# The recurrences of the chunk inverses issued on GpSimd instead of VectorE

## The chip, the cores and the metric

One core of one Trainium2 chip. The metric is the device time of one execution in microseconds (us). Engines are named as in the profile: PE is TensorE, PEld its weight loads, DVE is VectorE, ACT is ScalarE, POOL is GpSimd, SP is SyncE, which here issues most DMAs.

## What is computed

One layer of a hybrid decoder for a prompt of 1024 tokens and 8 samples of 4 tokens. All columns come from one product `x @ w_in`. A part of them feeds RWKV-7 time mixing, 8 heads of 64, which the reference runs token by token:

```python
def step(S, inp):
    r_t, w_t, k_t, v_t, kk_t, a_t = inp
    sa = jnp.einsum('bhvk,bhk->bhv', S, -kk_t)
    S = (S * w_t[:, :, None, :] + sa[..., None] * (kk_t * a_t)[:, :, None, :]
         + v_t[..., None] * k_t[:, :, None, :])
    return S, jnp.einsum('bhvk,bhk->bhv', S, r_t)
```

The other columns feed dilated window attention, gates, two output products, a last product and a layer norm. The change touches the time mixing of the prompt alone.

## The kernel before

The kernel takes the recurrence in chunks of 64 tokens. Inside a chunk the steps depend on each other through a strictly triangular 64x64 matrix, and the kernel needs the inverse of identity plus that matrix. The work is cut into 8 units: 4 pairs of heads (`j`) by 2 halves of the tokens (`hf`). A unit has 8 chunks and 2 heads, so 16 triangular matrices. Five streams make the first stage of the program, up to about 563 us:

- `products`: the columns of `x @ w_in`. Each 128 columns take two loads of weights (`load_w`, line L165 the load into `wraw`, L168 on ACT and L169 on DVE the split into `whi` and `wlo`) and 72 matmuls (L178). This is what PE does most of the time.
- `unit`: prepares a unit. It ends, for what matters here, with the masked matrices `AT` (L392, DVE, from PSUM tiles `g` that the matmuls of L385 write).
- `inverse`: the 32x32 diagonal blocks of the triangular matrices go to DRAM and back with another layout (`Yd`, L448; `Y`, L451, both issued on SP), and so 128 partitions each hold one row of work. Then 31 steps of forward substitution, r = 0 to 30: a product `tm` (L457) and a subtraction from `X` (L460) over m = r//4 + 1 rows of n = 31 - r elements, from 31 elements in the first to 8 in the last, at most 76. Each of the 62 operations needs the one before. At the end `X` goes back to DRAM (`Xd`, L464).
- `scan`: reads the inverted blocks back into `AT` (L478, SP), transposes them with DVE into `T1` (L479; the profile writes it `T`), joins the halves with small matmuls (L492, L502), and then goes chunk by chunk through the state: matmul L543, `W` on DVE (L544), matmul L549, the new state `st` on DVE (L552).
- `norms`: the output norm of a unit.

Two things set the order. `run_streams` deals the streams' pieces out by due times (`D_INV`, `D_IN` and the like), and PE executes exactly in that order (`manual_schedule`). On the other engines and in the DMA queues a scheduler chooses the order by its own estimate of when each instruction is ready. Once chosen it is fixed: every engine and every queue executes its own list in order, and an instruction that waits holds up all that stand behind it.

PSUM is scarce: the tiles `g` and `sc` have two banks each, `pj` four.

Of the kernel before, what the change touches and what calls it, by code (L numbers as in the profile page):

```python
# [15 lines left out]
ALU = mybir.AluOpType  # L16
# [68 lines left out]
def tile_layer(ctx: ExitStack, tc: tile.TileContext, A: dict, O: list):  # L85
    nc = tc.nc
    V, S, G, T, SP = nc.vector, nc.scalar, nc.gpsimd, nc.tensor, nc.sync
# [10 lines left out]
    def mk(pool, shape, tag, bufs=None, dt=F32):  # L98
        uid[0] += 1
        return pool.tile(list(shape), dt, tag=tag, name=f"{tag}_{uid[0]}", bufs=bufs)  # L100
# [216 lines left out]
    def unit(j, hf, M, st, out):  # L317
# [45 lines left out]
            yield None  # L363
        Mr = M[0]
        E = mk(rp, [P, 8, 65], "E", 2)
        G.memset(E[:, :, 0:1], 1.0)
        S.activation(E[:, :, 1:65], lam.rearrange("p (a b) -> p a b", a=8), AF.Exp, scale=-0.5 * CDEC)
        Ev = E.rearrange("p (a b) c -> p a b c", b=2)
        KR = mk(rp, [P, 4, 4, 64], "KR", 2)
# [72 lines left out]
    def inverse(j, hf, AT, out):  # L442
        Yd = mk(dpool, [2, 2, 2, 4, 32, 32], f"Yd{j}{hf}")
        Xd = mk(dpool, [2, 2, 2, 4, 32, 32], f"Xd{j}{hf}")
        blk = lambda p, b, w: AT[64 * (1 - p) + 32 * b : 64 * (1 - p) + 32 * b + 32, w, p::2, 64 * (1 - p) + 32 * b : 64 * (1 - p) + 32 * b + 32]
        for p in range(2):
            for b in range(2):
                SP.dma_start(Yd[p, b].rearrange("e c j i -> j e c i"), blk(p, b, slice(0, 2)))  # L448
        Y = mk(rp, [P, 32, 32], "Y", 1)
        for q in range(4):  # L450
            SP.dma_start(Y[32 * q : 32 * q + 32], Yd.rearrange("p b e c j i -> (p b e c) j i"))  # L451
        X = mk(rp, [P, 8, 32], "X", 1)
        SP.dma_start(X[:], A["cst"][:, XI0:].rearrange("p (a b) -> p a b", a=8))
        for r in range(31):
            m, n = r // 4 + 1, 31 - r
            tm = mk(rp, [P, 80], "tm", 2)[:, 0 : m * n].rearrange("p (a b) -> p a b", a=m)
            V.tensor_tensor(  # L457
                tm, Y[:, r : r + 1, r + 1 : 32].to_broadcast([P, m, n]), X[:, 0:m, r : r + 1].to_broadcast([P, m, n]), ALU.mult
            )
            V.tensor_tensor(X[:, 0:m, r + 1 : 32], X[:, 0:m, r + 1 : 32], tm, ALU.subtract)  # L460
            if r % 2:
                yield (0.0, D_INV)
        for q in range(4):
            SP.dma_start(  # L464
                Xd.rearrange("p b e c (a q) i -> q (p b e c) a i", q=4)[q],
                X[32 * q : 32 * q + 32],
            )
        out.append((Xd, blk))
# [235 lines left out]
    def units():  # L704
        for u in range(8):
            j, hf = u // 2, u % 2
            while j not in pairs:
                yield None
            M, st = pairs[j]
            yield from unit(j, hf, M, st, ready)  # L710
            done["unit"] += 1
        while done["scan"] < 7:
            yield None
        yield from sample_rows()

    def inverses():
        for u in range(8):
            while len(masked) <= u:
                yield None
            yield 0.0, D_IN  # L720
            yield from inverse(*masked[u], inv)
            yield 0.0, D_UP
            done["inv"] += 1
# [753 lines left out]
```

## Time and profile before

| | |
|---|---|
| median of 3 runs | 1368.11 us (1365.16 to 1368.77) |
| the profiled execution | 1365.17 us, its span 1363.5 us, granted clock 0.993 |
| PE busy | 1331.7 us, 98% of the span |
| DVE busy | 804.4 us, 59% |
| ACT busy | 469.2 us, 34% |
| POOL busy | 67.0 us, 5% |
| L457 and L460 on DVE | 248 each, 210 and 209 ns |
| first and last of them | 77.3 us and 523.5 us |

The span is the time from the first to the last instruction, and 1.7 us of the execution lie around it. A timeline row reads: start, duration, engine (SPq means that SP's queue issues a DMA there, and the duration is the issue alone), line, operation, output <- inputs, shapes, count of merged instructions, and in brackets the idle time of the engine before it with what ended it. A row of waits reads: waiting engine and line, what it waited for, total us, times, longest.

### The profile page before, as it was taken

To read this page: it belongs to the slowest core of one execution; us is meant where nothing else is said; L and a number is where in the kernel's file an instruction comes from. 1 tells how busy PE (TensorE), PEld (TensorE's weight loads), DVE (VectorE), ACT (ScalarE), POOL (GpSimd) and SP (SyncE) were. 2 spreads that over 40 slices of the span, in tenths; PEclk is the share of its full clock that TensorE was granted. 3 is DMA by queue.
4 is the path that set the end of the run, shared out by engine and by line. 5 is a ranking of instruction groups with operands and counts; after the bars stand their busy time and mean duration, and the time that the engine had idled before them with its cause. 6 is when DMAs were issued, how large, how long until landed. Compare 5 with 4: busy or idle time off the path is not lost.

```text
span 1363.5 us, 25941 instructions
## 1 busy us (share of the span) xinstructions
PE 1331.7 (98%) x10101; PEld 1241.0 (91%) x10101; DVE 804.4 (59%) x2204; ACT 469.2 (34%) x1065; POOL 67.0 (5%) x82
## 2 busy tenths in 40 slices
PE   9999999999999999999999999999999999999997
PEld 7998999898988999999999999999999998899786
DVE  5677668786476855543554385437543844665565
ACT  5334344434443443422332323232332234132211
POOL 0000000000000000000000000000000000025100
PEclk9999999999999999999999999999999999899999
DMA  6122223122313233328545455555554666795221
GB/s 210 44 61 66 67 86 97 51 75 72 93 61 81 72 109 96 96 89 156 106 109 120 118 132 103 123 129 128 100 120 119 135 130 158 237 286 163 84 100 68
DMA packets 340151, 151.64 MB, mean 111 GB/s; under 512 B 188808, under 2 KB 329502, under 8 KB 339774
## 3 DMA queue, kind: packets, MB, share of 16 engines
q1 hardware_dynamic: 241150, 129.68, 35.0%
q10 hardware_dynamic: 98880, 20.32, 7.5%
q8 instruction: 79, 1.29, 0.4%
q14 instruction: 42, 0.34, 0.1%
HBM read 110.68 MB, written 38.97 MB: 110 GB/s over the span
## 4 chain that ended last, share of the span: by engine, by line
PE 82%; DVE 11%; DMA 3%; issue 1%; SPq 1%; ACT 1%; ACTq 0%; DVEq 0%
PE pj L178 60%; PE pj L1431 7%; PE o L985 2%; PE s L948 2%; DVE tm L457 1%; DVE X L460 1%; PE g L385 1%; PE t L968 1%; PE s L1067 1%; DMA wraw<-in_w_in_dram 1%; PE sc L543 1%; DMA cb<-cd 1%; DVE wlo L169 1%; DVE st L552 1%; PE sc L549 1%
## 5 line engine op out<-in xcount | busy, mean ns | idle before, releaser
L178 PE MATMUL pj<-xhi,whi 128*128 128x352 f32 x1848 | 398.3, 337 | 4.5 <-ACT xhi L1298 3.1
L178 PE MATMUL pj<-xhi,wlo 128*128 128x352 f32 x1848 | 386.1, 330 | 0.0
L178 PE MATMUL pj<-xlo,whi 128*128 128x352 f32 x1848 | 380.5, 327 | 0.0
L178 PEld LDWEIGHTS pj<-xhi,whi 128*128 128x128 f32 x1848 | 304.5, 190 | 20.7 <-issue 10.6
L178 PEld LDWEIGHTS pj<-xlo,whi 128*128 128x128 f32 x1848 | 309.2, 190 | 1.8 <-issue 0.7
L178 PEld LDWEIGHTS pj<-xhi,wlo 128*128 128x128 f32 x1848 | 307.1, 189 | 3.9 <-issue 2.3
L169 DVE TENSOR_TENSOR wlo<-wraw,whi 128x512 fp32r<-128x512 f32 x162 | 112.8, 697 | 89.6 <-ACT whi L168 88.8
L168 ACT ACTIVATE whi<-wraw 128x512 fp32r<-128x512 f32 x162 | 100.5, 625 | 132.5 <-PE pj L178 94.3
L958 ACT ACTIVATE Sm<-Sm,nm 128x128 f32<-128x128 f32 (+1 forms) x96 | 42.4, 442 | 101.8 <-DVE nm L955 101.8
L457 DVE TENSOR_TENSOR tm<-Y,X 128x60 f32<-128x60 f32 (+24 forms) x248 | 52.1, 210 | 10.5 <-DMA Y<-Yd 4.3
L460 DVE TENSOR_TENSOR X<-X,tm 128x60 f32<-128x60 f32 (+24 forms) x248 | 51.9, 209 | 6.0
L552 DVE SCALAR_TENSOR_TENSOR st<-sc,E,SD 64x64 f32<-64x64 f32 x128 | 36.1, 282 | 29.0 <-PE sc L549 27.3
L950 DVE CUSTOM_DVE_ANT_0 Sm<-s,cst 128x128 f32<-128x128 f32 (+1 forms) x96 | 29.2, 347 | 39.6 <-PE s L948 38.9
L1431 PE MATMUL pj<-wl,mh 128*128 128x512 f32 (+1 forms) x136 | 51.9, 382 | 0.0
L541 ACT ACTIVATE SD<-st,E 128x128 f32<-128x128 f32 x64 | 25.6, 401 | 70.5 <-DVE st L552 70.4
L811 POOL TENSOR_TENSOR kvp<-vv,kv 128x512 f32<-128x512 f32 x16 | 20.2, 1262 | 470.8 <-DVE Ss L819 386.7
L985 PE MATMUL o<-PT,Vt 128*128 128x128 f32 x280 | 38.7, 276 | 0.8 <-ACT PT L972 0.8
L948 PE MATMUL s<-k,q 128*128 128x128 f32 (+1 forms) x192 | 37.8, 326 | 1.1 <-DVE ml L950 1.1
L873 ACT ACTIVATE k<-pj 128x352 f32<-128x352 f32 (+1 forms) x36 | 16.2, 455 | 65.1 <-PE pj L178 60.9
L311 ACT ACTIVATE zt<-pj,der 128x352 f32<-128x352 f32 x48 | 26.5, 553 | 33.1 <-PE pj L178 27.8
L985 PEld LDWEIGHTS o<-PT,Vt 128*128 128x128 f32 x280 | 36.4, 191 | 1.5 <-ACT PT L972 1.1
L544 DVE TENSOR_TENSOR W<-sc,R 64x128 f32<-64x128 f32 x64 | 18.4, 288 | 29.5 <-PE sc L543 28.4
(325 smaller groups left out, 1699.4 us busy)
## 6 DMA issues: line engine op xcount, KB each, us to landing
wraw<-in_w_in_dram SPq DMA_DIRECT2D x146, 256.0 KB
gd<-zt SPq DMA_DIRECT2D x48, 176.0 KB
gt<-gd SPq DMA_DIRECT2D x48, 176.0 KB
vs<-bt ACTq DMA_DIRECT2D x48, 128.0 KB
kc<-in_cache_kv_g_dram SPq DMA_DIRECT2D x48, 128.0 KB
Vt<-vs ACTq DMA_DIRECT2D x12, 512.0 KB
cb<-cd SPq DMA_DIRECT2D x12, 512.0 KB
zd<-zt SPq DMA_DIRECT2D x24, 176.0 KB
```

The source lines that it names most:

```text
L168: S.activation(hi[:], raw[:], AF.Copy)
L169: V.tensor_tensor(lo[:], raw[:], hi.bitcast(F32)[:], ALU.subtract)
L178: T.matmul(out, w[wi][:, n % 4, :], x[:, n % 4, :], start=first and n == 0, stop=last and n == 11)
L311: S.activation(t[:], b[:], AF.Tanh, scale=0.5, bias=der[:, HB + col : HB + col + 1])
L457: V.tensor_tensor(tm, Y[:, r : r + 1, r + 1 : 32].to_broadcast([P, m, n]), X[:, 0:m, r : r + 1].to_broadcast([P, m, n]), ALU.mult)
L460: V.tensor_tensor(X[:, 0:m, r + 1 : 32], X[:, 0:m, r + 1 : 32], tm, ALU.subtract)
L552: V.scalar_tensor_tensor(S1[d, d], pS[d, d], E[d, c, 64:65], SD[d, d], ALU.mult, ALU.add)
L948: T.matmul(r, qT[:, i * P : (i + 1) * P], kT[:, keys[i][0] * P : keys[i][0] * P + n], start=True, stop=True)
L950: V.tensor_tensor_reduce(out=Sm[:, i, 0:n], in0=r, in1=m3 if g == 2 else m12[:, 256 - n : 256], scale=1.0, scalar=NEG, op0=ALU.add, op1=AL ...
L958: S.activation(Sm[:, i, 0:n], Sm[:, i, 0:n], AF.Exp, scale=SCALE, bias=nm[:, x : x + 1], accum_out=ml[:, g, 1, i : i + 1])
L985: T.matmul(po[:, (i % 4) * P : (i % 4 + 1) * P], st["Vt"][:, kb_, :], PT[:, n * P : (n + 1) * P], start=m == 0, stop=m == len(keys[i]) - 1,)
L1431: T.matmul(pb[:], a[:, k], wk, start=x == 0, stop=x == len(prods) - 1)
```

## The change

All 62 operations of each of the 8 inverses go to POOL. The clearing of the first column of `E`, a tile of the decays that `unit` builds (L366; the change's title calls what needs it kappa), goes from POOL to DVE.

```diff
-        G.memset(E[:, :, 0:1], 1.0)
+        V.memset(E[:, :, 0:1], 1.0)
...
         for r in range(31):
             m, n = r // 4 + 1, 31 - r
             tm = mk(rp, [P, 80], "tm", 2)[:, 0 : m * n].rearrange("p (a b) -> p a b", a=m)
-            V.tensor_tensor(
+            G.tensor_tensor(
                 tm, Y[:, r : r + 1, r + 1 : 32].to_broadcast([P, m, n]), X[:, 0:m, r : r + 1].to_broadcast([P, m, n]), ALU.mult
             )
-            V.tensor_tensor(X[:, 0:m, r + 1 : 32], X[:, 0:m, r + 1 : 32], tm, ALU.subtract)
+            G.tensor_tensor(X[:, 0:m, r + 1 : 32], X[:, 0:m, r + 1 : 32], tm, ALU.subtract)
```

PE's list is the same, row by row. The lists of DVE, SP and POOL change, and ACT's at a few places. First, DVE at the end of the first inverse, as a difference; a number behind a name tells one tile of that name from the next. `T_258_1425` is the first unit's `T1`, `AT_704` its matrices, `AT_1114` the second unit's matrices.

```order
-L457 TENSOR_TENSOR tm_1131<-Y_907,X_912 128x75
+L479 STREAM_TRANSPOSE T_258_1425<-AT_704 32x256
 L392 TENSOR_TENSOR AT_1114<-g_1150,cst_76 128x512
-L460 TENSOR_TENSOR X_912<-X_912,tm_1131 128x5x15
 L392 TENSOR_TENSOR AT_1114<-g_1151,cst_76 128x512
-L457 TENSOR_TENSOR tm_1134<-Y_907,X_912 128x70
-L460 TENSOR_TENSOR X_912<-X_912,tm_1134 128x5x14
-L457 TENSOR_TENSOR tm_1162<-Y_907,X_912 128x65
+L479 STREAM_TRANSPOSE T_258_1425<-AT_704 32x256
 L205 SCALAR_TENSOR_TENSOR zt_1176<-zt_1177,pj_1012 128x352
```

The transposes of the first unit now stand ahead of the last two maskings of the second unit; before, the recurrence was at its steps of 75 to 65 elements there, and the transposes came after its end.

Second, DVE at the third inverse. Before, the transposes of its unit (`T_545_2969`) stood here, after the second unit's whole loop over the chunks (`Ot_2343` is its output):

```order
L371 TENSOR_TENSOR KR_2922<-m_1235,E_2919 128x4x2x64
L564 TENSOR_TENSOR Ot_2343<-Ot_2343,g_2863 128x512
L574 TENSOR_REDUCE m_529_2898<-Ot_2343 128x8
L575 TENSOR_SCALAR m_529_2898<-m_529_2898 128x8
L576 TENSOR_TENSOR Ot_2343<-Ot_2343,m_529_2898 128x512
L479 STREAM_TRANSPOSE T_545_2969<-AT_2149 32x256
```

Now they stand inside that loop:

```order
L169 TENSOR_TENSOR wlo_2830<-wraw_2827,whi_2829 128x512
L552 SCALAR_TENSOR_TENSOR st_68_386<-sc_2675,E_1050,SD_2645 64x64 x2
L373 SCALAR_TENSOR_TENSOR t_2925<-m_1235,prm_96,t_2626 128x512
L479 STREAM_TRANSPOSE T_545_2969<-AT_2149 32x256
L544 TENSOR_TENSOR W_1205<-sc_2702,R_237_1303 64x128
L479 STREAM_TRANSPOSE T_545_2969<-AT_2149 32x256
L552 SCALAR_TENSOR_TENSOR st_67_385<-sc_2727,E_1050,SD_2700 64x64 x2
L544 TENSOR_TENSOR W_1205<-sc_2763,R_237_1303 64x128
```

`W` and `st` of the sixth to the eighth chunk of the second unit, which stood ahead of the transposes before, are behind them now. The other units are alike: the eighth unit's transposes now stand between `st` and `W` of the seventh unit's loop.

Third, SP's queue at the first inverse, as a difference:

```order
 L165 DMA wraw_1475<-in_w_in_dram 128x4x128
+L464 DMA Xd_149_902<-X_912 256x1x32 x4
 L165 DMA wraw_1581<-in_w_in_dram 128x4x128
+L478 DMA AT_704<-Xd_149_902 32x8x32 x4
 L206 DMA zd_95<-zt_1141 128x352
+L453 DMA X_1617<-in_cst_dram 128x256
 L448 DMA Yd_281_1606<-AT_1114 32x8x32 x2
```

The transfers of the finished `X` went ahead of a load of weights, of the stores `zd` and of the second unit's `Yd`, behind which they stood before. On POOL the eight inverses follow each other; between them stand only the clearings of `st` for the third and fourth pair (L681, after the third and the fifth inverse) and, after the sixth, three operations of the sample rows (L631, L646, L647).

## The prediction

> **What bounds the kernel now.** I read the page first, then the windows of the first stage, then PE's waits, then the timeline around single inverses. The page:
>
> ```profile
> PE 1331.7 (98%) x10101; PEld 1241.0 (91%) x10101; DVE 804.4 (59%) x2204; ACT 469.2 (34%) x1065; POOL 67.0 (5%) x82
> ```
>
> PE bounds the whole. The next fence has two stretches, that of the eight inverses and the third inverse's 30 us: length, busy time of PE, PEld, DVE, ACT and POOL, clock, DMA share and rate. Then the same for tile X alone (DVE), and PE's waits in the long stretch.
>
> ```profile
> 77.00:525.00 448.00, 434.37 (x3936) 405.71 (x3935) 321.48 (x1124) 187.97 (x397) 2.83 (x14) 0.99 0.27 76
> 194.00:224.00 30.00, 28.98 (x213) 27.30 (x212) 27.21 (x108) 13.02 (x30) 0.20 (x1) 1.00 0.23 72
> ...
> 77.00:525.00 448.00, 104.03 (x496) 0.99 0.27 76
> 194.00:224.00 30.00, 12.99 (x62) 1.00 0.23 72
> ...
> PE sc L543 <- DVE st L552: 6.9, 8, 2.3
> PE sc L492 <- DVE T L479: 3.3, 3, 2.1
> PE sc L549 <- DVE W L544: 2.3, 3, 1.1
> PE g L385 <- DVE BK L360: 0.5, 1, 0.5
> PE g L385 <- DVE AT L392: 0.4, 1, 0.4
> ```
>
> DVE gives up 104.03 of 321.48 us. But PE is idle for 448.00 - 434.37 = 13.6 us only, 13.4 of them by these waits for DVE. So a lighter DVE can win 13 us at most. What can be lost depends on when each inverse ends, since the transposes L479 that read its result now stand far earlier in DVE's list, ahead of work that PE needs.
>
> **How long an inverse takes on POOL.** No row shows these operations there. The nearest are other products and sums:
>
> ```profile
> 380.88 0.40 POOL L631 TENSOR_TENSOR m<-sM,prm 128x128 f32<-128x128 f32 x1 [23.34 <-PE g L413]
> ...
> 548.64 0.42 POOL L643 TENSOR_TENSOR m<-t,der 128x128 f32<-128x128 f32 x1 [72.48 <-ACT t L626]
> 549.14 0.42 POOL L644 TENSOR_TENSOR m<-m,der 128x128 f32<-128x128 f32 x1
> 549.63 0.47 POOL L645 TENSOR_TENSOR m<-m,sM 128x128 f32<-128x128 f32 x1
> ...
> 681.35 1.04 POOL L811 TENSOR_TENSOR kvp<-vv,kv 128x512 f32<-128x512 f32 x1 [16.27 <-DVE Ss L819]
> 703.94 1.55 POOL L811 TENSOR_TENSOR kvp<-vv,kv 128x512 f32<-128x512 f32 x1 [21.55 <-DVE Ss L819]
> ...
> 1229.51 0.95 POOL L1324 TENSOR_TENSOR xhi<-xhi,gt 128x352 f32<-128x352 f32 x1 [0.99 <-DVE gt L1323]
> 1231.44 1.50 POOL L1324 TENSOR_TENSOR xhi<-xhi,gt 128x352 f32<-128x352 f32 x1 [0.99 <-DVE gt L1323]
> ...
> L811 POOL TENSOR_TENSOR kvp<-vv,kv 128x512 f32<-128x512 f32 x16 | 20.2, 1262 | 470.8 <-DVE Ss L819 386.7
> L366 POOL MEMSET E<- 128x8 f32 x8 | 0.9, 112 | 286.9 <-DVE st L552 286.9
> ```
>
> Products with a broadcast input, as L457: 0.40 us at 128 elements, 1.04 at 512, so 1.67 ns an element and 0.19 us fixed. Sums in place, as L460: 0.47 at 128, 0.95 at 352, so 2.1 ns and 0.20 us. The code's m times n over 31 steps makes 1560 elements. The products take 31 x 0.19 + 1560 x 0.00167 = 8.5 us, the subtractions 31 x 0.20 + 1560 x 0.0021 = 9.5. Each needs the one before, and L643 to L645, such a chain, start 0.50 and 0.49 us apart with durations of 0.42: a hand-over of 0.08, 62 of them 5.0 us. Sum 23.0 us, with DVE out of the way.
>
> DVE is not quite out of the way: L811 and L1324 take 1.04 and 0.95 us, or half a microsecond more. L811's mean is 1.262, 21% over its least. That on 18.0 us of operations, for the two thirds of the inverse in which DVE works, is 2.5 us. I take 25 us. Low end: the fixed part of a tiny operation is at least L366's 0.11, so 62 x 0.11 + 5.9 + 5.0 = 17.7 us. High end: DVE's other work in the third inverse's window, (27.21 - 12.99)/30 of the time, stops POOL altogether while DVE still has work (193.5 to 215.3 us below): 23.0 + 0.47 x 21.8 = 33.2 us. The rows of whole operations on POOL are nearest, hence 25.
>
> [...]
>
> **What waits for it.** With order as in the change, three inverses worked out (first, third, eighth):
>
> ```profile
> 70.41 1.76 SPq L451 DMA_DIRECT2D Y<-Yd  x4
> ...
> 97.82 0.68 DVE L392 TENSOR_TENSOR AT<-g,cst 128x512 f32<-128x512 f32 x1
> ...
> 99.05 1.02 PE L405 MATMUL g<-t,cst 128*128 128x512 f32 x2
> ```
>
> ```profile
> 185.00 0.78 SPq L451 DMA_DIRECT2D Y<-Yd  x2
> ...
> 188.80 1.74 SPq L451 DMA_DIRECT2D Y<-Yd  x2
> ...
> 214.51 0.75 DVE L373 SCALAR_TENSOR_TENSOR t<-m,prm,t 128x512 f32<-128x512 f32 x1
> ...
> 215.42 0.28 DVE L544 TENSOR_TENSOR W<-sc,R 64x128 f32<-64x128 f32 x1
> ...
> 216.44 0.38 PE L549 MATMUL sc<-W,BT 128*128 128x128 f32 x2
> ```
>
> ```profile
> 497.89 0.90 SPq L451 DMA_DIRECT2D Y<-Yd  x2
> ...
> 501.73 0.19 DVE L457 TENSOR_TENSOR tm<-Y,X 128x31 f32<-128x31 f32 x1 [0.35 <-DMA Y<-Yd]
> ...
> 523.51 0.17 DVE L460 TENSOR_TENSOR X<-X,tm 128x8 f32<-128x8 f32 x1
> ...
> 525.79 0.29 DVE L544 TENSOR_TENSOR W<-sc,R 64x128 f32<-64x128 f32 x1 [0.64 <-PE sc L543]
> ...
> 527.52 0.38 PE L549 MATMUL sc<-W,BT 128*128 128x128 f32 x2
> ...
> 531.11 0.43 DVE L479 STREAM_TRANSPOSE T<-AT 32x256 f32<-32x256 f32 x1
> ```
>
> The eighth gives two lags: the recurrence started 501.73 - 498.79 = 2.9 us after the last issue of Y, as soon as it had landed, and L479 came 531.11 - 523.68 = 7.4 us after the last subtraction (through Xd and back). Both stay.
>
> - Third: Y ready at 188.80 + 1.74 + 2.9 = 193.4, inverse done at 218.4, transposes possible at 225.8. DVE is at them when L373 ends, 215.3, so it stands still for 10.5 us. Behind them is W; PE's L549 can start at 225.8 + 0.43 + 0.28 = 226.5 instead of 216.4: PE loses 10.1.
> - First: ready 72.2 + 2.9 = 75.1, done 100.1, transposes at 107.5, then two maskings of 0.68, 109.3. PE's L405 needs a bank that they free and stood at 99.05: 10.3.
> - Eighth: ready 501.7, done 526.7, transposes 534.1, W 534.8; L549 stood at 527.5: 7.3.
>
> Mean 9.2 us. The other five are alike in order, so 8 x 9.2 = 74 us. Each loss comes alone: the next unit's masking, and so its inverse, moves along with PE.
>
> Against it: of the 13.4 us of waits the 3.3 for L479 go, since it comes earlier against PE, and about half of the others, 5, as DVE is lighter: -8. The issues of Y in the third inverse, 5.5 us from first to last against 1.76 in the first, wait for other things in SP's queue; a lighter DVE frees them by 0 to 2 us, taken as 1: -8. Sum +58 us (74 - 16).
>
> The rest at nothing: the eight clearings of E, 0.11 us each, on a DVE that has gaps. On SP, Xd now stands ahead of loads of weights. In the first inverse the third of the three loads below, issued at 95 us before, comes after Xd, at 100.1 + 3.3 = 103.4, some 9 us later. The loads' lead covers it:
>
> ```profile
> 77.39 17.70 SPq L165 DMA_DIRECT2D wraw<-in_w_in_dram  x3
> ...
> 194.44 0.40 SPq L165 DMA_DIRECT2D wraw<-in_w_in_dram  x1
> ...
> 213.77 0.69 DVE L169 TENSOR_TENSOR wlo<-wraw,whi 128x512 fp32r<-128x512 f32 x1
> ...
> 223.19 3.30 SPq L464 DMA_DIRECT2D Xd<-X  x4
> ```
>
> The load at 194.44 and the split at 213.77 belong together by count (28th load, 28th split): 19 us lie between. If that cover went, the loads would be next to hold PE. What stood behind the recurrence on DVE gains up to its 13.0 us; nothing on POOL stands behind an inverse that PE needs sooner than the next one.
>
> The profiled execution took 1365.17 us, so 1365.17 + 58 = 1423; the runs' median lies 3 us above it, so 1425.
>
> **Rivals.** A, faster: an inverse of 17 us or less. Every stall above then shrinks by 8 us or more, to about 1, and the -16 outweighs it: 8 x 1 - 16 = -8, or 1357 us. The point is an inverse of 17.8 us, where 8 x (9.2 - 7.2) = 16. For it: L366's 0.11 us. Against: every product on POOL has 0.40 or more, and hand-overs alone are 5 us.
>
> B, longer: POOL and DVE shut each other out. 32 us an inverse, 7 more than mine, 8 x 7 = 56 us more: 1480. For it: 1.55 against 1.04 us. Against: DVE stands still in the last third. [...]
>
> C, no change: PE has other work while DVE stands still, so that a wait in DVE's list doesn't reach it. Against: PE's list is in order and L549 sits 1 us behind W. It needs 18 us an inverse, or stalls below 2 us: 1367.
>
> **Chances.** Forecast 0.78, A 0.06, B 0.11, C 0.05. Slower by over 0.3% (4 us, about what a measurement here can tell) is the forecast and B, 0.89; same 0.05; faster 0.06. The range goes from an inverse of 20 us (1425 - 8 x 5 = 1385) to 31 us (1425 + 8 x 6 = 1473).
>
> **What would show it.** After: 248 of L457 at about 0.27 us and of L460 at 0.30 on POOL, first to last of an inverse 25 us; DVE idle some 10 us before each L479, put down to the transfer of AT; PE waiting eight times 7 to 10 us, mostly L549 or L543 for W or st and once L405; PE busy unchanged, DVE near 700. Wrong if an inverse is 18 us or less, or if L479 comes late with PE busy throughout.

## The result, and the profile after

The changed kernel takes 1446.7 us (median, 1444.5 to 1449.2) against 1367.0 us (1365.2 to 1368.8): a ratio of 1.059, 95% interval 1.057 to 1.061. It is slower by 80 us, where the prediction had 58 (1425, range 1385 to 1473).

First the page's row of busy times. Then the two stretches (stage of the inverses, rest), in the columns explained above; before, they were 448.00 us with 434.37 of PE and 838.50 with 823.54. Then the groups of the moved operations and of the transposes: count, busy us in all, mean ns, idle time ahead of them and what ended it. Last, PE's waits.

```profile
PE 1344.9 (93%) x10101; PEld 1254.4 (87%) x10101; DVE 724.4 (50%) x1716; ACT 471.3 (33%) x1065; POOL 234.6 (16%) x570
```

```profile
77.00:608.00 531.00, 450.54 (x3959) 421.81 (x3959) 243.37 (x639) 191.81 (x402) 170.16 (x501) 0.92 0.23 66
608.00:1443.80 835.80, 820.09 (x5671) 764.20 (x5669) 438.34 (x969) 244.78 (x599) 62.66 (x58) 0.99 0.51 128
```

```profile
L457 POOL TENSOR_TENSOR tm<-Y,X 128x60 f32<-128x60 f32 (+24 forms) x248 | 81.4, 328 | 341.8 <-DMA Y<-Yd 323.0
L460 POOL TENSOR_TENSOR X<-X,tm 128x60 f32<-128x60 f32 (+24 forms) x248 | 87.7, 354 | 19.4
L479 DVE STREAM_TRANSPOSE T<-AT 32x256 f32<-32x256 f32 x16 | 6.9, 433 | 76.3 <-DMA AT<-Xd 76.2
```

```profile
PE sc L543 <- DVE st L552: 43.8, 8, 11.7
PE sc L549 <- DVE W L544: 23.5, 5, 9.2
PE g L405 <- DVE AT L392: 11.5, 1, 11.5
```

All of the loss lies in the stage of the inverses: it is 83.0 us longer, the rest 2.7 shorter. Of the 83.0, 66.8 are idle time of PE (80.5 us against 13.6) and 16.2 are busy time. A part of that are 23 more matmuls that fall into the stretch; over the whole run PE is busy 13.2 us longer with the same matmuls (1344.9 against 1331.7), at a granted clock of 0.92 in this stage where it had 0.99. DVE is 80 us lighter (724.4 against 804.4). That is less than the 104 us of the moved operations, because before their rows overlapped other rows of DVE in part, and because other operations of DVE now take some 5 us longer (last section). DVE stood still for 76.2 us ahead of L479, and of the 78.8 us of PE's waits shown here 73.4 are eight stalls: 11.5, 6.4, 9.2, 8.2, 8.9, 11.7, 10.6 and 6.9 us, unit by unit.

The third inverse shows the chain. Its first and last operation on POOL, DVE's list at its end, and PE:

```profile
211.90 0.24 POOL L457 TENSOR_TENSOR tm<-Y,X 128x31 f32<-128x31 f32 x1 [63.80 <-DMA Y<-Yd]
...
237.69 0.21 POOL L460 TENSOR_TENSOR X<-X,tm 128x8 f32<-128x8 f32 x1
```

```profile
233.23 0.75 DVE L373 SCALAR_TENSOR_TENSOR t<-m,prm,t 128x512 f32<-128x512 f32 x1
244.15 0.44 DVE L479 STREAM_TRANSPOSE T<-AT 32x256 f32<-32x256 f32 x1 [10.17 <-DMA AT<-Xd]
244.62 0.28 DVE L544 TENSOR_TENSOR W<-sc,R 64x128 f32<-64x128 f32 x1
```

```profile
244.96 0.80 PE L549 MATMUL sc<-W,BT 128*128 128x128 f32 x2 [9.22 <-DVE W L544]
```

DVE is through with L373 at 233.98 and waits 10.17 us, since L479 is next in its list. W, which belongs to the unit before and needs nothing of this inverse, comes behind it, and PE waits 9.22 us for W. From first to last operation an inverse takes 25.9 us on average on POOL; on DVE, among DVE's other work, it took 28.9. So the inverse became shorter and the kernel 6% slower.

### The profile page after: what moved, and what is told of

The parts are those of the page before. It is cut to its first block, busy times and chain, and to the rows that moved or that the text cites. A ratio compares the mean times of both kernels' runs of the same rounds, so it can differ in the third digit from the quotient of the medians.

```text
span 1443.8 us, 25935 instructions
## 1 busy us (share of the span) xinstructions
PE 1344.9 (93%) x10101; PEld 1254.4 (87%) x10101; DVE 724.4 (50%) x1716; ACT 471.3 (33%) x1065; POOL 234.6 (16%) x570
## 4 chain that ended last, share of the span: by engine, by line
PE 68%; POOL 12%; DMA 8%; issue 4%; SPq 3%; DVE 3%; ACT 1%; POOLq 0%; ACTq 0%; DVEq 0%
PE pj L178 50%; PE pj L1431 6%; POOL X L460 6%; POOL tm L457 6%; PE s L948 2%; PE o L985 2%; DMA Y<-Yd 2%; DMA cb<-cd 1%; PE g L385 1%; DMA Xd<-X 1%; PE t L968 1%; SPq L464 1%; PE s L1067 1%; DMA AT<-Xd 1%; DMA cd<-nE 1%
## 5 line engine op out<-in xcount | busy, mean ns | idle before, releaser
L178 PE MATMUL pj<-xhi,wlo 128*128 128x352 f32 x1848 | 392.3, 334 | 0.0
L178 PEld LDWEIGHTS pj<-xhi,wlo 128*128 128x128 f32 x1848 | 311.9, 192 | 4.5 <-issue 2.9
L178 PEld LDWEIGHTS pj<-xlo,whi 128*128 128x128 f32 x1848 | 313.1, 192 | 1.8 <-issue 0.7
L169 DVE TENSOR_TENSOR wlo<-wraw,whi 128x512 fp32r<-128x512 f32 x162 | 113.8, 704 | 117.1 <-ACT whi L168 116.2
L168 ACT ACTIVATE whi<-wraw 128x512 fp32r<-128x512 f32 x162 | 100.5, 625 | 132.8 <-PE pj L178 93.9
L457 POOL TENSOR_TENSOR tm<-Y,X 128x60 f32<-128x60 f32 (+24 forms) x248 | 81.4, 328 | 341.8 <-DMA Y<-Yd 323.0
L460 POOL TENSOR_TENSOR X<-X,tm 128x60 f32<-128x60 f32 (+24 forms) x248 | 87.7, 354 | 19.4
L543 PE MATMUL sc<-st,KR 128*128 128x128 f32 x128 | 27.6, 299 | 43.8 <-DVE st L552 43.8
L543 PEld LDWEIGHTS sc<-st,KR 128*128 128x128 f32 x128 | 23.2, 202 | 48.3 <-issue 43.7
L549 PE MATMUL sc<-W,BT 128*128 128x128 f32 x128 | 27.0, 294 | 23.5 <-DVE W L544 23.5
L549 PEld LDWEIGHTS sc<-W,BT 128*128 128x128 f32 x128 | 23.0, 200 | 27.2 <-DVE W L544 25.5
L479 DVE STREAM_TRANSPOSE T<-AT 32x256 f32<-32x256 f32 x16 | 6.9, 433 | 76.3 <-DMA AT<-Xd 76.2
```

The costliest lines, as they stand in the source:

```text
L168: S.activation(hi[:], raw[:], AF.Copy)
L169: V.tensor_tensor(lo[:], raw[:], hi.bitcast(F32)[:], ALU.subtract)
L178: T.matmul(out, w[wi][:, n % 4, :], x[:, n % 4, :], start=first and n == 0, stop=last and n == 11)
L457: G.tensor_tensor(tm, Y[:, r : r + 1, r + 1 : 32].to_broadcast([P, m, n]), X[:, 0:m, r : r + 1].to_broadcast([P, m, n]), ALU.mult)
L460: G.tensor_tensor(X[:, 0:m, r + 1 : 32], X[:, 0:m, r + 1 : 32], tm, ALU.subtract)
L543: T.matmul(pr[:, 0:P], KR[:, c2, 2 * p : 2 * p + 2, :], S0[:], start=True, stop=True)
```

## The experiments

The theory: PE loses its time because W and st, or the maskings, stand behind L479 in DVE's list. Rivals: the work on POOL slows DVE and ACT; the result of the inverse comes too late for the work that needs it (L492); the clearing of E is late; SP's queue, where Xd waits for POOL.

### L479 put back in DVE's list

```diff
-            V.transpose(T1[...], AT[...])
+            behind(V.transpose(T1[...], AT[...]), last["st"] if "st" in last else last["mask"])
```

`behind` gives the scheduler an order and no wait.

> The changed kernel, with one thing altered: L479 of a unit stands in DVE's list behind the last st (L552) of the unit before it (of the first unit: behind the second unit's last masking L392), as it did in the kernel before. All 62 operations of an inverse stay on POOL, the clearing of E stays on DVE, and the lists of PE, ACT, SP and POOL are word for word those of the changed kernel. Theory (PE stalls because W and st stand behind a transpose that waits for POOL): the eight stalls of 6 to 12 us go, PE is idle for 5 to 15 us in the stretch of the inverses instead of 80.5, the granted clock there is back at 0.99 since nothing stops PE, and the time is 1350 to 1366 us, most likely 1357. Rival (POOL's traffic slows DVE and with it PE, or the inverse on POOL is simply too late for the work that needs its result): order changes nothing of that, so 1430 us or more. Mixed case: the stalls go, but the clock stays at 0.92 because it is POOL's load that lowers it: about 1372 us.

Measured: 1421.5 us, ratio 1.040 (1.038 to 1.042). Better by 25 us, not by 80: neither theory nor rival. PE's waits, and the third inverse again on SP's queue, ACT, DVE and PE:

```profile
PE sc L543 <- DVE st L552: 42.3, 9, 10.4
PE g L423 <- DVE bon L406: 10.3, 1, 10.3
PE sc L549 <- DVE W L544: 5.0, 2, 4.3
```

```profile
213.82 0.38 SPq L165 DMA_DIRECT2D wraw<-in_w_in_dram  x1
228.51 2.51 SPq L464 DMA_DIRECT2D Xd<-X  x4
232.43 1.82 SPq L478 DMA_DIRECT2D AT<-Xd  x4
234.29 0.45 SPq L165 DMA_DIRECT2D wraw<-in_w_in_dram  x1
234.78 0.50 SPq L312 DMA_DIRECT2D gd<-zt  x1
```

```profile
238.09 0.55 ACT L311 ACTIVATE zt<-pj,der 128x352 f32<-128x352 f32 x1 [10.76 <-DMA gd<-zt]
238.54 0.62 ACT L168 ACTIVATE whi<-wraw 128x512 fp32r<-128x512 f32 x1
```

```profile
239.19 0.69 DVE L169 TENSOR_TENSOR wlo<-wraw,whi 128x512 fp32r<-128x512 f32 x1 [10.55 <-ACT whi L168]
239.92 0.60 DVE L552 SCALAR_TENSOR_TENSOR st<-sc,E,SD 64x64 f32<-64x64 f32 x2
```

```profile
240.66 0.77 PE L543 MATMUL sc<-st,KR 128*128 128x128 f32 x2 [8.24 <-DVE st L552]
```

The same fault sits in a second list. SP issues nothing from 214.2 to 228.5, because Xd is next and POOL is not done. Behind it stand a load of weights and the stores `gd`. ACT waits 10.76 us for a store to free a buffer of `zt`, so `whi` is late, so `wlo` on DVE, and st behind that. In the changed kernel the two waits ran at the same time, and PE's waits named only the one on DVE. SP's rows of that kernel show the other:

```profile
223.69 0.38 SPq L165 DMA_DIRECT2D wraw<-in_w_in_dram  x1
237.93 2.52 SPq L464 DMA_DIRECT2D Xd<-X  x4
```

SP stood still there from 224.07 to 237.93, and over the whole run L464 waited 143.5 us for POOL. (The first unit's 10.3 us, for bon, are still DVE's own: there L479 stands behind the last masking only, and DVE waits for it.)

### The clearing of E alone

In the kernel before, `G.memset(E[...])` becomes `V.memset(E[...])`.

> The kernel before, with the other part of the change alone: the eight clearings of E (L366) on DVE, the inverses still on DVE. Theory: eight times about 0.1 us on an engine with gaps, so no change, 1367 us within 4. Rival (the clearing, which the next unit's maskings need, is what comes late on DVE): a good part of the 80 us, 1390 us or more.

Measured: 1366.2 us, ratio 0.9999 (0.9991 to 1.0008). This part of the change costs nothing, as expected.

### A shorter and a longer inverse, the lists as in the changed kernel

```diff
+            if r % 3 < 2:
                 G.tensor_tensor(tm, ...)
                 G.tensor_tensor(X[...], X[...], tm, ALU.subtract)
```

```diff
-            G.tensor_tensor(tm, ...)
+            for again in range(1 + (r < 20)): G.tensor_tensor(tm, ...)
```

> The changed kernel with every third step of the inverse left out (r = 2, 5, ... 29: ten products and ten subtractions of 31 each, so X is not the whole inverse), and L479 held between the same W and st of DVE's list as in the changed kernel. Left out are 513 of 1560 elements and 20 of 62 operations, about 8.2 us of 25.9 for each inverse. Theory: each stall of PE shrinks by that much or to nothing: of 11.5, 6.4, 9.2, 8.2, 8.9, 11.7, 10.6 and 7 us some 11 us in all are left, and 1446 - 63 = 1383 us at an unchanged clock of 0.92, about 1372 if the clock recovers with the stalls. Rival (POOL's load slows DVE all the time): the loss shrinks with the work, by a third, to about 1420 us.

> The changed kernel with each of the first 20 products of an inverse (r below 20) done twice into the same tile, and L479 held between the same W and st of DVE's list as in the changed kernel. 20 operations and 1130 elements more: by the measured rows 20 x 0.27 + 1130 x 0.0017 = 7.3 us, with contention about 8 us more per inverse. Theory: each of the eight stalls grows by the whole of it, 64 us, and the lower clock behind stalls adds some 10 to 15: 1510 to 1525 us. Rival (POOL's load slows DVE all the time): the loss of 80 us grows by about a third, with the work, to about 1473 us.

The shorter one leaves out every third step and so does not compute the whole inverse. Measured: 1382.9 us (ratio 1.012, 1.010 to 1.014) and 1508.7 us (1.104, 1.103 to 1.106), at inverses of 18.0 and 33.4 us. PE's waits, short and then long:

```profile
PE sc L543 <- DVE st L552: 14.4, 8, 4.7
PE g L405 <- DVE AT L392: 4.2, 1, 4.2
PE sc L549 <- DVE W L544: 4.0, 2, 3.5
```

```profile
PE sc L543 <- DVE st L552: 73.8, 8, 18.1
PE sc L549 <- DVE W L544: 48.6, 5, 17.7
PE g L405 <- DVE AT L392: 19.3, 1, 19.3
```

7.9 us less took 63.8 us off the time, 7.5 us more added 62.0. The rival that POOL's load slows everything in proportion gave 1420 and 1473, and is out.

In the long kernel all of the 62 us is waiting: each of the eight stalls grew, by 6.4 to 9.2 us, so all eight inverses are on PE's path, with 8.3 us for each microsecond of an inverse. PE is busy for 1344.0 us, no more than the changed kernel's 1344.9; the 10 to 15 us that were expected for the clock did not come, and 1508.7 lies just below the expected 1510 to 1525. Against the kernel before (1331.7) that is 12.3 us more of busy time with stalls of 14 to 19 us, and 13.2 with stalls of 6 to 12: in these two kernels the price of the lower clock is paid by the stall, not by its length.

In the short kernel the spans differ by 63.6 us, of which 8.8 are busy time that came back with the clock (1336.1 against 1344.9) and 54.8 are waiting, since stalls of 6.4 and 6.9 us cannot shrink by 7.9. That the expected 1383 was met is therefore partly luck: it was worked out with an unchanged clock and 11 us of stalls left, and the waits above come to 22.6.

### Both lists put right

L479 as in the first experiment, and on SP, from a table of the counts in the kernel before, each L464 and L478 `behind` as many loads of weights and stores of `zt` as there.

> The kernel of the first experiment (L479 behind the loop of the unit before, inverses on POOL), and on SP's queue the transfers of the finished X (L464 and L478) held behind the same number of weight loads (L165) and of stores of zt (L206, L312) as in the kernel before. Theory as it now stands (two lists hold PE: DVE's by L479, and SP's by Xd, which waits for POOL ahead of loads and stores; in the changed kernel the two waits run at the same time): with both put right PE is idle for 5 to 15 us in the stretch of the inverses, the granted clock there is 0.98 or more, and the time is 1350 to 1366 us, most likely 1357. Rival (the result of an inverse on POOL, sent off later, is late for the products L492 that read it): new waits of PE for T, 1375 to 1400 us. Rival (POOL's load slows what DVE and ACT do for PE): no better than the 1421 us of the first experiment.

Measured: 1362.8 us, ratio 0.9974 (0.9962 to 0.9987), all inverses on POOL. Stage of the inverses, and PE's waits:

```profile
77.00:522.00 445.00, 433.74 (x3944) 407.42 (x3941) 240.16 (x634) 190.81 (x401) 169.95 (x501) 0.99 0.27 77
...
PE sc L543 <- DVE st L552: 6.0, 5, 1.8
PE sc L492 <- DVE T L479: 4.5, 3, 2.3
```

The whole loss is gone, the clock is back at 0.99, and PE's idle time is 11.3 us. So it was order in two lists. The load of POOL costs PE nothing that can be seen: on DVE some operations of the preparation do take longer with the inverses on POOL (L359 and L360, 771 and 762 ns in the changed kernel where they had 686 and 680), but here L169, the split that PE waits for, has a mean of 697 ns over the run as before. This kernel is faster than the changed one by 84 us, and than the one before by 2.3 us (0.3%; the interval leaves 1 out, narrowly).

### One list at a time, and POOL's own queue

First the changed kernel's order on DVE, but Xd and AT issued by POOL, which was meant to leave nothing on SP that waits for POOL: `G.dma_start` for `SP.dma_start` in L464 and L478. Then the same with L479 put back.

> The changed kernel with L479 held between the same W and st of DVE's list as there, and the transfers of the finished X (L464) and back into AT (L478) issued from POOL's own queue instead of SP's, so that nothing on SP stands behind a wait for POOL. Theory: DVE's list alone is enough for the whole loss; the eight stalls of PE stay at 6 to 12 us, changed only by what an issue from POOL adds to the 7 us from the last subtraction to L479 (each microsecond of it 8 us): 1440 to 1470 us. Rival (it was SP's queue that made the changed kernel slow, and DVE's list only looked like it): 1375 us or less.

> The kernel of the first experiment (L479 behind the loop of the unit before, inverses on POOL), with the transfers of the finished X (L464) and back into AT (L478) issued from POOL's own queue instead of SP's. SP's queue then holds no wait for POOL at all. Theory: the stalls of 4 to 10 us that the first experiment still had go, 1350 to 1366 us, most likely 1357, as with the transfers held back on SP. How long an issue from POOL takes no row shows yet; up to some 10 us more per inverse lie within the time between the end of an inverse and the end of the loop that L479 waits for. Rival (what the first experiment still lost was POOL's load on memory and not SP's queue): about 1421 us.

Measured: 1456.3 us (ratio 1.067, 1.064 to 1.069) and 1411.8 us (1.034, 1.032 to 1.037). PE's waits in the first:

```profile
PE sc L543 <- DVE st L552: 47.6, 8, 13.8
PE sc L549 <- DVE W L544: 27.6, 4, 12.4
PE g L405 <- DVE AT L392: 11.6, 1, 11.6
```

The second missed its 1357: SP waited for POOL after all, for another transfer, the start value that is loaded into the one buffer of X (L453). SP's waits in the second:

```profile
SPq L453 <- DMA Xd<-X: 116.6, 14, 25.9
```

The first has the same wait on SP, 114.8 us, so its list of SP is not free either. It still shows what DVE's list does alone. In seven units SP issues L453 3.1 to 5.9 us before L479 starts, so that the end of the stall is DVE's. In the eighth, where no start value follows, nothing on SP waits for POOL, and PE waits 6.7 us for W all the same (6.9 in the changed kernel). So DVE's list is enough for the whole loss; a run with that list and SP wholly free was not made.

Then L453 went to POOL's queue too, with L479 put back as in the second.

> The kernel that issues Xd (L464) and the transfers back into AT (L478) from POOL's queue, with L479 behind the loop of the unit before; now the loading of the next unit's start value into X (L453) is issued from POOL's queue as well, behind L478. There is one buffer for X, so on SP this load waited for Xd, with loads of weights and stores of zt behind it (116.6 us of SP's waits). Theory (the 1412 us were SP's queue again, held by L453 in the place of L464): PE's stalls of 4 to 12 us go, 1355 to 1368 us, most likely 1361. Rival (issuing transfers from POOL is itself what hurts): 1400 us or more.

Measured: 1387.9 us, ratio 1.015 (1.013 to 1.018), which again missed its 1355 to 1368. Half of the rest went, not all. What is left is DVE's list at three units (the first, fourth and seventh) where L479, though behind the loop, still stands ahead of work of PE's and comes late:

```profile
109.51 0.43 DVE L479 STREAM_TRANSPOSE T<-AT 32x256 f32<-32x256 f32 x1 [11.03 <-DMA AT<-Xd]
```

```profile
297.27 0.43 DVE L479 STREAM_TRANSPOSE T<-AT 32x256 f32<-32x256 f32 x1 [4.70 <-DMA AT<-Xd]
```

```profile
493.93 0.43 DVE L479 STREAM_TRANSPOSE T<-AT 32x256 f32<-32x256 f32 x1 [7.44 <-DMA AT<-Xd]
```

```diff
+AFTER = ("BK", 2), ("st", 0), ("st", 1), ("norm", 2), ("st", 3), ("st", 4), ("norm", 5), ("st", 6)
...
+    [behind(last["T", u, p], last[k]) for u, k in enumerate(AFTER) for p in range(2)]
```

> The kernel that issues Xd, the transfers into AT and the start value of X from POOL's queue (1388 us), with three pairs of transposes L479 moved further back in DVE's list and nothing else: the first unit's behind BK of the third unit (L360), the fourth's behind the norm of the third (L585), the seventh's behind the norm of the sixth. In its trace these three are the places where L479 still stood ahead of work of PE's: DVE was idle for 11.0, 4.7 and 7.4 us ahead of them, and PE waited 10.2 us for bon and 8.0 + 1.7 us for AT and KR. Theory (what is left of the loss is again DVE's list): these 20 us of PE go, with some 5 us of lower clock, so 1358 to 1366 us, most likely 1362; not much below, since PE's waits would then be about those of the kernel with both lists put right (1362.8). Rival (transfers issued from POOL cost the rest): 1380 us or more.

Measured: 1365.2 us, ratio 0.9994 (0.9981 to 1.0007), as expected. With those three pairs moved, and nothing else, the rest of the loss is gone, and transfers issued by POOL cost nothing either.

### A longer inverse where the lists are right

The first 20 products done twice again, now in the kernel with both lists put right, and in the last one.

> The kernel with both lists put right (L479 behind the loop of the unit before, Xd and AT on SP behind the same loads and stores as in the kernel before), with each of the first 20 products of an inverse done twice, as in the run that made the changed kernel's inverse longer (1446.7 to 1508.7 us, 62 us). Theory (the length of an inverse counts only where a list stands still behind it): the first unit, whose products L492 already wait for T, loses the whole 8 us and the others a part at most, so 1371 to 1385 us. Rival (the length of an inverse on POOL counts by itself): 62 us here too, about 1425 us.

> The kernel of the run beside this one, with each of the first 20 products of an inverse done twice, as in the two longer runs before (62 us more for the changed kernel, 37 more for the kernel with both lists put right, which on SP still had loads behind Xd). Theory (the length of an inverse counts only for what stands in line behind it, and beyond the time between AT's landing and L492): by the trace of the 1388 us kernel AT lands 19, 34, 24, 19, 21 and 18 us ahead of L492 in six units and 5 and 4 us ahead in the third and the sixth, so with 7.5 us more only these two lose, 3 to 4 us each, with the clock some 10 us in all: 8 to 16 us above the run beside it, about 1373 us. Rival (the length on POOL counts by itself): 60 us above it.

Measured: 1400.5 us, 37.7 more than without, and 1388.0 us, 22.8 more; both above what was expected, and far below the 62 of the changed kernel. In the first, SP's list still has work behind Xd, as at the seventh inverse, where ACT then waits for a store (`gd`) that stands behind Xd, and the split `whi` (L168) stands behind that on ACT (SP's rows, then ACT's):

```profile
478.47 0.38 SPq L165 DMA_DIRECT2D wraw<-in_w_in_dram  x1
491.68 2.86 SPq L464 DMA_DIRECT2D Xd<-X  x4
496.16 0.34 SPq L453 DMA_DIRECT2D X<-in_cst_dram  x1
497.08 0.92 SPq L312 DMA_DIRECT2D gd<-zt  x2
...
500.40 0.55 ACT L311 ACTIVATE zt<-pj,der 128x352 f32<-128x352 f32 x1 [4.86 <-DMA gd<-zt]
```

In the second, PE's new waits are these:

```profile
PE g L385 <- DVE KR L371: 6.9, 2, 3.5
PE g L385 <- DVE AT L392: 4.9, 1, 4.9
```

Two of 3.4 and 3.5 us in the third and the sixth unit, as expected, and one of 4.9 in the seventh, which was not. With 8.2 us more of busy time they make 20.0, against 19.6 us between the spans. So the length of an inverse is hidden in five units of eight, and does not count by itself.

## Why the prediction was right, and where its numbers were off

- **Inverse on POOL, 25 us:** 25.9 us. The operations take 81.4 + 87.7 = 169.1 us, 21.1 an inverse, against 18.0 and 2.5 for contention; the hand-overs are the remaining 4.8 us (5.0). One of the two rows for sums in place (L645, 0.47 us) is by the kernel's text a product; the sum beside it, L644, took 0.42, with which the subtractions would have been put at 7.3 us an inverse instead of 9.5. They took 11.0 and the products 10.2 (8.5), so the good total is in part luck. In the third inverse the first product (31 elements) took 0.24 us and the last subtraction (8 elements) 0.21, which is what the rows of other operations on POOL had given. Rivals A (17 us) and B (32 us) are out, and C with them, since PE did wait. That POOL and DVE shut each other out, as B has it, no run shows; POOL's operations did take longer with DVE at work beside them, but by little: with the least duration of each shape they would take 17.2 us an inverse, so about 3.9 of the 21.1 are that (last section).
- **Stalls by L479 in DVE's list, 10.3, 10.1 and 7.3 us for the first, third and eighth unit, 74 in all:** 11.5, 9.2 and 6.9, and 73.4 in all. PE waited for W, st and once for g, as forecast, and DVE stood still 9.5 us on average ahead of L479. The rule by which the stalls were worked out, that each ends one microsecond later for each microsecond of the inverse, measured 8.3 us for eight in the longer kernel. That the sum fits to 0.6 us is luck: by that rule the 0.9 us of a longer inverse alone make 7 us, and the five units that were only said to be alike had 6.4 to 11.7 us.
- **PE's waits of before that go, -8:** the idle time beside the eight stalls is 80.5 - 73.4 = 7.1 us, where it was 13.6: -6.5.
- **Earlier issue of Y, -8:** this step failed as forecast. In the third inverse the issues of Y took 5.5 us before (185.00 to 190.54) and take 5.0 after (204.62 to 209.60). In both runs a store (`yd`, L596) stands between the second and the third of them. Over the eight units 0 to 0.6 us were gained in seven, and 5.3 us in the second (7.0 to 1.7 us). That one gain is already in the stalls above, where the second unit has the shortest, 6.4 us.
- **PE busy unchanged:** this step failed too, and it is the largest miss: PE is busy 13.2 us longer, by the clock (0.92 in the stage of the inverses where it had 0.99; last section), a term that the prediction put at nothing without a reason. With it the sum is 73.4 - 6.5 + 13.2 = 80.1 us, the measured 80.3 between the spans. The forecast of 58 had no such term and 8 us for Y taken off.
- **E's clearings at nothing:** right, 0.9999.
- **Xd ahead of the loads on SP at nothing, by a lead of 19 us:** right for the sum by luck, and wrong in its reason. SP's list was worth some 45 us as soon as DVE's no longer covered it (1421.5 against 1362.8, less the first unit's stall and its clock). What covered it was not the lead of the loads but the stall on DVE, which ran at the same time; and besides loads there were stores behind Xd, whose buffers ACT waited for. The lead was read at one unit and one kind of transfer.
- **A lighter DVE can win 13 us at most:** with both lists right the gain is 2.3 us. 11.3 us of PE's idle time stay, since st and T still stand behind other work of DVE's: the preparation of the next unit. The longest wait for st there, 1.78 us up to 330.71, has L357, L359 and L360 between the two operations of st on DVE, as has the same wait of 2.26 us in the kernel before. The longest wait for T, 2.33 us up to 120.46, has L353, L359 and L357 ahead of L479.
- **DVE near 700 us:** 724.4, for the overlap of rows told with the result.

## What to carry to other kernels

When work goes to an idle engine, look in every list that holds a consumer of its result, the DMA queues too, for what stands behind that consumer: the price is there. Here the moved work even became shorter (25.9 us against 28.9), and the kernel slower. Two such waits can run at the same time, so that the waits of the engine that counts name one, and taking it away shows the other; the gain of one repair is then no measure of its cause. An instruction that waits for a far engine belongs behind everything in its list that needs nothing of it, up to the point where its own result is due.

## What the runs showed of the hardware

In the changed kernel each of PE's eight long stalls is paid for a second time, by the clock (13.2 us in all). The third of them, with PE's busy time and, third from the end of a row, the granted clock:

```profile
238.00:239.00 1.00, 0.00 (x0) 0.00 (x0) 0.00 (x0) 0.00 (x0) 0.00 (x0) 0.99 0.00 0
239.00:244.00 5.00, 0.00 (x0) 0.00 (x0) 0.00 (x0) 0.00 (x0) 0.00 (x0) 0.50 0.27 43
244.00:245.00 1.00, 0.04 (x1) 0.04 (x1) 0.72 (x2) 0.06 (x1) 0.00 (x0) 0.50 0.39 64
245.00:249.00 4.00, 4.00 (x14) 4.00 (x15) 1.00 (x3) 2.02 (x5) 0.00 (x0) 0.50 0.63 185
249.00:250.00 1.00, 1.00 (x7) 1.00 (x7) 0.40 (x2) 0.31 (x2) 0.00 (x0) 0.89 0.43 153
250.00:254.00 4.00, 4.00 (x28) 4.00 (x27) 1.26 (x4) 0.57 (x2) 0.02 (x1) 1.00 0.25 72
```

PE stopped at 235.7 and resumed at 244.96. The clock fell to one half 3.2 us after the stop and came back 4.3 us after the restart: 14 matmuls in 4 us where 28 follow. Half of 4.3 us is lost, about 2 us a stall, 17 us for eight by this one (an estimate), against 13.2 measured. Stalls of 14 to 19 us (the longer inverse) cost no more of it (PE busy for 1344.0 us against 1344.9), and the load on POOL has no part in it, since the clock is 0.99 with both lists put right and POOL at work for 169.95 us of that stage.

At the other seven stalls the clock fell 2.0 to 4.1 us after the stop and came back 3.9 to 6.0 us after the restart. In windows of 0.25 us the eight stretches at half clock last 6.8 us (one), 10.2 (four) or 13.7 (three). In the kernel before, stalls of 2.15 and 2.26 us were each followed by a stretch of 3.41 us at half clock, which began 1.1 and 1.2 us after PE had resumed, with PE at work throughout. Half of that is 1.7 us a stall; from these two the prediction's eight stalls would have had some 14 us more (an estimate). In the very last run, the longer inverse with the lists right, three new stalls of 3.4, 3.5 and 4.9 us came with 8.2 us more of busy time (1340.2 against 1332.0). So the price is a mean of 1.7 us for the eight stalls (13.2 by 8) and of 2.7 for these three (8.2 by 3).

POOL's operations take longer with DVE at work beside them. In the changed kernel the products, with least, median and longest duration in ns:

```profile
L457 POOL TENSOR_TENSOR tm<-Y,X x248: 206/286/1103, 75.9 to 596.2; 128x60 f32<-128x60 f32 x12, 128x54 f32<-128x54 f32 x8, 128x66 f32<-128x66 f32 x8, 128x28 f32<-128x28 f32 x8
```

Their mean of 328 ns compares with 274 (8.5 us for 31), the estimate from the rows without contention. Set beside DVE's rows, 236 of the 496 operations have no work of DVE's beside them, and together they take 0.5 us more than the least duration of their shape; the other 260 take 30.7 us more, 3.8 us an inverse. The longest, of 1.10 to 1.14 us where the least is about 0.3, lie beside L343, an operation of 1.23 us on DVE.

DVE's side shows a little of it. L359 and L360 went from 686 and 680 ns to 771 and 762, L357 from 686 to 745, L353 from 684 to 729 (8 each). L169 has 704 instead of 697 over the run. In all this is some 5 us of DVE's 724.4.
